# A gated linear attention's gate, projected with tokens on the partitions and multiplied before the transpose

## The chip, the cores and the metric

The kernel runs on one core of a Trainium2 chip. The metric is the device time of one execution in microseconds (us), taken as the median of several runs. A separate execution is recorded by the hardware profiler; its rows name engines as PE (TensorE matmul), PEld (TensorE weight load), DVE (VectorE), ACT (ScalarE), POOL (GpSimd) and SP (SyncE, which issues most DMAs). L94 is line 94 of the kernel.

## The reference

Two layers. Each projects x (256 tokens, 2048 wide) and feeds three groups of heads: A, banded softmax attention of 8 heads; B, gated linear attention (GLA) of 4 heads; M, cross-attention of 4 heads into 256 memory tokens. Each group's output is multiplied by a SiLU gate that is itself a projection of x. The concatenation goes through one output projection, and a layer norm closes the layer. Cut to what matters here:

```python
h = x @ w_in                                   # a_q a_k a_v a_z  b_q b_k b_v b_z b_lr  m_q m_z
y_a = chunk_band_attention(a_q, a_k, a_v)      # 8 heads of 128
o_b = gla_chunk_recurrence(b_q, b_k, b_v, log_g)          # (B, S, 4 heads, 128)
o_b = o_b * rsqrt(mean(square(o_b), axis=-1) + RMS_EPS) * gla_norm_g
y_b = o_b.reshape(B, S, B_WIDTH)               # 512 wide
y_m = memory_attention(m_q, mk, mv)            # 4 heads of 128
y = concatenate([y_a * silu(a_z), y_b * silu(b_z), y_m * silu(m_z)])
x = layer_norm(DEEPNORM_ALPHA * x + y @ w_out)
```

## The kernel before, in words

All matrices are float32. For the large products each operand is split into a high and a low part of the matmul type float32r (`parts`: ACT rounds the high part at L117, DVE subtracts at L118), and three products are added: high times high, low times high, high times low. An operand with features on the partitions is a tile of the pool `opp` (`operand()`, five tiles); four of them hold the layer's x.

Weights come in pieces of 1024 columns of float32 per partition (`piece`): SP loads `raw`, ACT and DVE make `wh` and `wl`; each of the three tags has four buffers. A projection of 512 columns has one of two forms. `ws_group` holds the weights still and streams x, so its result has features on the partitions: two halves of 256 features, each of four pieces (`ws_half`), with two 512-wide and two 256-wide matmuls for each of the 16 blocks of 128 rows and each half. `as_group` holds x still and streams the weights, so its result has tokens on the partitions: eight pieces, with three 512-wide matmuls for each block and each 128 tokens.

The result of a half of `ws_group`, or of a whole `as_group`, is an accumulator `acc` of two PSUM banks from the pool `psd`, which has two of them; the other four banks are the pool `psa` (`bank()`), for the heads. A half is evacuated by `total`: ACT reads one part (L258), DVE adds the other (L259).

PE and SP follow the program's order; ACT, DVE and POOL are put in order by the scheduler that builds the program. The heads are generators that run between the pieces: each piece ends with `tick()`, which takes the next step of a generator that is due.

```python
while waiting and len(active) < 2:
    active.append((waiting.pop(0), 0))
```

At most two are active, the others stand in the list `waiting` in the order they came: the GLA, eight heads of A, four heads of M. A step that yields n is due again n ticks later. `finish` ticks until given generators are done.

In each layer the groups follow one another so: memory keys and values, the GLA's query and key, then values, queries and keys of A, the query of M (MQ), then the four gates BZ, AZ0, AZ1 and MZ, all in the `ws_group` form, then four blocks of the output projection in the `as_group` form. Under the gates run the last heads: the heads of M have three steps each (`m_head`, scores and softmax, transposes, values). The last block of the output projection takes each piece in two DMAs, from a layout split in two parts of 256 columns.

The GLA ends with tokens on the partitions: two tiles `on` of scratch get the outputs (L443), the mean squares (L445), and the factor of the norm (L451); eight transposes (L457) turn them, and ACT multiplies by the norm's gain while it copies them into `yraw` (L459). After a gate group, ACT takes the Silu (L768), DVE multiplies by `yraw` (L772), and `parts` makes the operand of the output projection.

Of the kernel before, what the change touches and what calls it, by code (L numbers as in the profile page):

```python
# [8 lines left out]
F32 = mybir.dt.float32  # L9
# [3 lines left out]
AF = mybir.ActivationFunctionType  # L13
ALU = mybir.AluOpType
# [4 lines left out]
P = 128  # L19
D = 2048  # L20
T = 256
# [11 lines left out]
G_MK, G_MV, G_BQK, G_AQ0, G_AK0, G_AQ1, G_AK1, G_MQ, G_BZ, G_AZ0, G_AZ1, G_MZ, G_WO = range(13)  # L33
# [4 lines left out]
def hybrid_trunk_kernel(  # L38
# [7 lines left out]
    pe, dve, act, pool, sp = nc.tensor, nc.vector, nc.scalar, nc.gpsimd, nc.sync  # L46
# [4 lines left out]
    waiting, active, done, now = [], [], set(), [0]  # L51

    def tick():

        now[0] += 1
        while True:
            while waiting and len(active) < 2:
                active.append((waiting.pop(0), 0))
            due = [e for e in active if e[1] <= now[0]]
            if not due:  # L60
                return
            active.remove(due[0])
            g = due[0][0]
            after = next(g, None)
            if after is not None:
                active.append((g, now[0] + after))
                return
            done.add(g)

    def finish(gens):  # L70
        while not all(g in done for g in gens):
            tick()
# [16 lines left out]
    def nm(s):  # L89
        uid[0] += 1  # L90
        return f"{s}_{uid[0]}"
# [4 lines left out]
    def bank():  # L96
        return psa.tile([P, 512], F32, name=nm("bk"), tag="bk")

    def scratch(shape, dtype=F32):
        return sc.tile(shape, dtype, name=nm("sc"), tag="sc")  # L100

    def small(shape, tag, bufs=1):
        return sm.tile(shape, F32, name=nm(tag), tag=tag, bufs=bufs)

    ident = cst.tile([P, P], F32, name="ident")
# [4 lines left out]
    def operand():  # L110

        x = opp.tile([P, 4, 2, T], F32R, name=nm("x"), tag="x")
        return x[:, :, 0], x[:, :, 1], x.rearrange("p j h t -> p j (h t)")

    def parts(hi, lo, src):

        act.copy(hi, src)  # L117
        dve.tensor_tensor(lo, src, hi.bitcast(F32), op=ALU.subtract)  # L118

    def load_quarter(src):  # L120

        with tc.high_priority(AHEAD):
            raw = wp.tile([P, 4, T], F32, name=nm("raw"), tag="raw")
            x = operand()
            sp.dma_start(raw, src)
            parts(x[0], x[1], raw)
        return x

    def piece(src, n, kp=2):

        with tc.high_priority(AHEAD):
            raw = wp.tile([P, kp, n], F32, name=nm("raw"), tag="raw")
            hi = wp.tile([P, kp, n], F32R, name=nm("wh"), tag="wh")
            lo = wp.tile([P, kp, n], F32R, name=nm("wl"), tag="wl")
            if isinstance(src, list):
                w = n // len(src)
                for i, part in enumerate(src):
                    sp.dma_start(raw[:, :, i * w:(i + 1) * w], part.rearrange("p (k n) -> p k n", k=kp))
            else:
                sp.dma_start(raw.rearrange("p k n -> p (k n)"), src)  # L140
            parts(hi, lo, raw)
        return hi, lo
# [108 lines left out]
    def ws_group(src, xq):  # L251

        for half in range(2):
            acc = ws_half(src[half * 4:half * 4 + 4], xq)
            yield half * 2, acc[:, :, 0], acc[:, :, 1]

    def total(dst, a, b, scale=1.0):
        act.mul(dst, b, scale)  # L258
        dve.scalar_tensor_tensor(dst, a, scale, dst, op0=ALU.mult, op1=ALU.add)  # L259

    def as_products(o, t, xq, w, kt, kk):
        wh, wl = w
        xh, xl, _ = xq[kt // 4]
        j, ts = kt % 4, slice(t * P, (t + 1) * P)
        mm(o, xh[:, j, ts], wh[:, kk], kt == 0, False)
        mm(o, xl[:, j, ts], wh[:, kk], False, False)
        mm(o, xh[:, j, ts], wl[:, kk], False, kt == 15)

    def as_group(src, xq, n, kp=2, first=None):

        acc = psd.tile([P, 2, 512], F32, name=nm("acc"), tag="acc")
        for pc in range(16 // kp):
            if first is not None and pc % 2 == 0:
                xq.append(load_quarter(first[pc // 2]))
            w = piece(src[pc], n, kp)
            for kk in range(kp):
                for t in range(2):
                    as_products(acc[:, t, :n], t, xq, w, pc * kp + kk, kk)
            tick()
        return acc  # L280
# [12 lines left out]
    def gla_inputs(l):  # L293
        gw = small([16, 256], "gw")
        gb = small([P, 2], "gb")
        ng = small([P, 1], "ng")
        pool.dma_start(gw, gate_w[l])
        pool.dma_start(gb, gate_b[l])
        pool.dma_start(ng, norm_g[l])
        return gw, gb, ng  # L300

    def gla(gw, gb, ng, gq, gk, asv, yraw):
# [23 lines left out]
        pt = bank()  # L326
# [53 lines left out]
        pt = bank()  # L380
# [8 lines left out]
        for c in range(3):  # L389
            rs = slice((c % 2) * 64, (c % 2) * 64 + 64)  # L390
            t = c // 2
            for b in range(2):
                for par in range(2):
                    h = 2 * b + par
# [4 lines left out]
        for c in range(3):  # L399
            t = c // 2  # L400
# [17 lines left out]
                ps = slice(half * CH, (half + 1) * CH)  # L418
                act.copy(attn[par][ps, :, ps], pairs[par][ps])
        yield 3  # L420
        on = [scratch([P, 4, P]) for _ in range(2)]
        ms = small([P, 8], "ms")
        sq = scratch([P, P])

# [2 lines left out]
        for par in range(2):  # L427
            for t in range(2):
                for b in range(2):
                    h = 2 * b + par  # L430
                    mm(po[par][:, (t * 2 + b) * P:(t * 2 + b + 1) * P], attn[par][:, t * 2 + b],
                       asv[:, t, 16 + h * P:16 + (h + 1) * P], t == b == 0, False)
        for odd, even in ((1, 2), (3, None)):
            for b in range(2):
                for c in (odd, even):
                    if c is not None:
                        for par in range(2):
                            rs = slice(par * 64, par * 64 + 64)
                            g = (c // 2) * 2 + b
# [9 lines left out]
        rsqrt(rr, ms, 8, 1)  # L449
        for par in range(2):  # L450
            dve.tensor_tensor(on[par], on[par], rr[:, par * 4:par * 4 + 4].unsqueeze(2).to_broadcast([P, 4, P]), op=ALU.mult)  # L451
        yield 2
        for par in range(2):
            pt = bank()
            for t in range(2):
                for b in range(2):
                    pe.transpose(pt[:, b * T + t * P:b * T + (t + 1) * P], on[par][:, t * 2 + b], ident)  # L457
            for b in range(2):
                act.activation(yraw[:, 2 * b + par], pt[:, b * T:(b + 1) * T], AF.Copy, scale=ng[:, 0:1])  # L459

    SCALE = P ** -0.5

# [71 lines left out]
    def transposed(xq):  # L534

        for q in range(4):
            x = operand()
            hi, lo, _ = x
            xq.append(x)
            for j in range(0, 4, 2):  # L540
                pt = bank()
                for jj in range(2):
                    kt = q * 4 + j + jj
                    for t in range(2):
                        pe.transpose(pt[:, jj * T + t * P:jj * T + (t + 1) * P], res[:, t, kt * P:(kt + 1) * P], ident)  # L545
                parts(hi[:, j:j + 2], lo[:, j:j + 2], pt.rearrange("p (j t) -> p j t", j=2))
                yield 2

    def columns(n):
        return slice(n * 512, (n + 1) * 512)  # L550
# [133 lines left out]
    for l in range(L):  # L684
        mk = [per.tile([P, 4, T], F32R, name=nm("mk"), tag=f"mk{i}") for i in range(2)]
        mv = [per.tile([P, 2, 512], F32R, name=nm("mv"), tag=f"mv{i}") for i in range(2)]
        xq = []
# [6 lines left out]
        else:  # L694
            memq = []
            parts(*mv, as_group(w512[l, G_MV], memq, 512, 2, memT))
            gens = [transposed(xq)]
# [7 lines left out]
        yraw = [per.tile([P, 4, T], F32, name=nm("yr"), tag=f"yr{i}") for i in range(4)]  # L705
# [4 lines left out]
        gp = gla_inputs(l)  # L710
# [31 lines left out]
        load_bias(0)  # L742
        load_bias(1)
        gens = [[gla(*gp, gq, gk, asv, yraw[0])]]
        waiting.extend(gens[0])
        for half in range(2):
# [11 lines left out]
        waiting.extend(gens[-1])  # L758


        yq = []
        for i, g in enumerate((G_BZ, G_AZ0, G_AZ1, G_MZ)):
            y = operand()
            gates = []
            for j, a, b in ws_group(w512[l, g], xq):
                sz = scratch([P, 2, T])
                total(sz, a, b)
                act.activation(sz, sz, AF.Silu)  # L768
                gates.append((j, sz))
            finish(gens[i])  # L770
            for j, sz in gates:
                dve.tensor_tensor(sz, sz, yraw[i][:, j:j + 2], op=ALU.mult)  # L772
                parts(y[0][:, j:j + 2], y[1][:, j:j + 2], sz)
            yq.append(y)


        last = l == L - 1
# [3 lines left out]
        for n in range(WO_N):  # L781
            g, b = scratch([P, 512]), scratch([P, 512])
# [19 lines left out]
            acc = as_group(src, yq, 512)  # L802
            for t in range(2):
                add_residual(n, t, acc[:, t], stats)
            if last:
                for t in range(2):
                    r = res[:, t, columns(n)]
# [89 lines left out]
```

## Time and profile before

| | us |
|---|---|
| median of 3 runs | 939.01 (938.53 to 939.02) |
| the profiled execution | 938.5 |
| its span, first to last instruction | 936.4 |
| mean granted TensorE clock | 0.994 of full |

How to read the rows. A row of the timeline has its start in us from the span's start, its length, the engine, the line, the operation, what it writes and reads, shapes and a count, and in brackets how long the engine had been idle before and what released it. Matmul lengths are modelled and overlap, so the distance between two starts is the better measure of pace. A row of the waits has engine, line and what it waited for, then the total, the count and the longest. A row of the windows has the stretch, its length, the busy time and count of PE, PEld, DVE, ACT and POOL, the granted clock, the DMA share and GB/s. In the chain that ended last PE has most of the span, and DMAs were 57.5% of the sixteen engines' time.

### The profile page before, as it was taken

The page shows a single profiled execution, that of the slowest core. Times are in us where ns is not written, and L with a number is a line of the kernel's source. Part 1 is how long each engine was busy: PE and PEld are TensorE (multiplying, and loading weights), DVE is VectorE, ACT ScalarE, POOL GpSimd, SP SyncE. Part 2 cuts the span into 40 slices and gives each one's busy share as a digit, 9 for nine tenths or more (in the row PEclk, how much of TensorE's full clock was granted, in tenths as well). Part 3 has the DMA queues.
Part 4 walks back from the last instruction along what each step waited for, and adds up shares of the span by engine and source line. Part 5 has one row for each costly group of instructions (what it writes and reads, how often), then busy time and mean ns, then how long its engine had stood idle before and what let it go on. Part 6 is the DMA issues. An engine that isn't in the chain of part 4 may idle for free.

```text
span 936.4 us, 14232 instructions
## 1 busy us (share of the span) xinstructions
PE 926.8 (99%) x5520; PEld 813.9 (87%) x5520; DVE 585.6 (63%) x780; ACT 497.8 (53%) x714; POOL 30.1 (3%) x46
## 2 busy tenths in 40 slices
PE   9999999999999999999999999999999999999996
PEld 7889998998888888888888999889888888888884
DVE  5764487555565666555598445965555667566666
ACT  6644474475456665434465346744745576554340
POOL 1000000000000000000041000000000001010000
PEclk9999999999999999999999999999999999999997
DMA  8956855555554466765756475556555554676642
GB/s 290 340 187 175 305 189 168 159 180 175 191 159 157 157 183 199 250 198 183 237 190 225 140 208 177 196 161 186 162 195 163 169 160 155 194 247 204 196 135 90
DMA packets 64723, 178.75 MB, mean 191 GB/s; under 512 B 7016, under 2 KB 22664, under 8 KB 64400
## 3 DMA queue, kind: packets, MB, share of 16 engines
q1 hardware_dynamic: 62928, 173.56, 57.5%
q0 software_dynamic: 1728, 4.28, 1.8%
q8 instruction: 43, 0.70, 0.3%
q14 instruction: 24, 0.20, 0.1%
HBM read 175.69 MB, written 2.10 MB: 190 GB/s over the span
## 4 chain that ended last, share of the span: by engine, by line
PE 94%; DVE 2%; DMA 2%; issue 1%; ACT 0%; SPq 0%; DVEq 0%
PE acc L94 85%; PE bk L94 8%; DMA raw<-memT 1%; PE bk L486 1%; DVE wl L118 0%; PE bk L521 0%; PE bk L545 0%; DVE stats L561 0%; ACT x L117 0%; DVE res L580 0%; DVE res L648 0%; DMA raw<-w 0%; DVE res L560 0%; PE bk L457 0%; DVE x L118 0%
## 5 line engine op out<-in xcount | busy, mean ns | idle before, releaser
L118 DVE TENSOR_TENSOR wl<-raw,wh 128x1024 fp32r<-128x1024 f32 (+3 forms) x325 | 378.3, 1166 | 272.4 <-ACT wh L117 267.9
L117 ACT CAST wh<-raw 128x1024 fp32r<-128x1024 f32 (+3 forms) x325 | 323.3, 996 | 352.9 <-PE acc L94 243.1
L94 PE MATMUL acc<-x,wh 128*128 128x512 f32 x1376 | 439.4, 401 | 0.0
L94 PE MATMUL acc<-wh,x 128*128 128x512 f32 (+1 forms) x1120 | 321.8, 368 | 0.4 <-ACT wh L117 0.4
L94 PEld LDWEIGHTS acc<-x,wl 128*128 128x128 f32 x1376 | 258.4, 188 | 61.2 <-DVE wl L118 0.4
L94 PE MATMUL acc<-x,wl 128*128 128x256 f32 x1376 | 271.4, 279 | 0.0
L94 PEld LDWEIGHTS acc<-wh,x 128*128 128x128 f32 x1120 | 206.1, 188 | 25.5 <-ACT wh L117 1.6
L94 PEld LDWEIGHTS acc<-x,wh 128*128 128x128 f32 x1376 | 211.9, 189 | 2.4 <-issue 0.3
L94 PE MATMUL acc<-wl,x 128*128 128x512 f32 (+1 forms) x560 | 205.8, 368 | 0.1
L94 PEld LDWEIGHTS acc<-wl,x 128*128 128x128 f32 x560 | 105.2, 188 | 13.2 <-DVE wl L118 1.3
L478 ACT ACTIVATE sc<-sc,mx 128x128 f32<-128x128 f32 (+1 forms) x32 | 14.4, 449 | 18.4 <-DVE mx L476 18.4
L259 DVE SCALAR_TENSOR_TENSOR sc<-acc,sc 128x512 f32<-128x512 f32 x23 | 15.7, 683 | 0.0
L471 DVE SCALAR_TENSOR_TENSOR sc<-bk,bias 128x384 f32<-128x384 f32 x16 | 8.9, 555 | 10.8 <-PE bk L94 10.8
L772 DVE TENSOR_TENSOR sc<-sc,yr 128x512 f32<-128x512 f32 x16 | 11.0, 690 | 6.4 <-ACT sc L768 6.4
L560 DVE SCALAR_TENSOR_TENSOR res<-res,acc 128x512 f32<-128x512 f32 x15 | 9.7, 684 | 7.2 <-PE acc L94 7.2
L258 ACT ACTIVATE sc<-acc 128x512 f32<-128x512 f32 x23 | 13.7, 595 | 0.0
L118 DVE TENSOR_TENSOR x<-res,x 128x512 fp32r<-128x512 f32 (+2 forms) x14 | 10.5, 765 | 5.1 <-ACT x L117 5.1
L94 PE MATMUL bk<-qk,qk 128*128 128x128 f32 (+1 forms) x64 | 13.1, 326 | 0.0
L94 PE MATMUL bk<-sc,asv 128*128 128x256 f32 (+1 forms) x64 | 13.0, 326 | 0.0
L768 ACT ACTIVATE sc<-sc 128x512 f32<-128x512 f32 x16 | 10.1, 630 | 4.6 <-DVE sc L259 4.5
L94 PEld LDWEIGHTS bk<-sc,asv 128*128 128x128 f32 x64 | 11.0, 189 | 0.8
L117 ACT CAST x<-res 128x512 fp32r<-128x512 f32 (+2 forms) x14 | 9.2, 679 | 4.7 <-DMA res<-xT 3.2
(175 smaller groups left out, 541.2 us busy)
## 6 DMA issues: line engine op xcount, KB each, us to landing
raw<-w SPq DMA_DIRECT2D x230, 512.0 KB, 3.6
raw<-w SPq DMA_DIRECT2D x64, 388.0 KB, 3.1
raw<-w SPq DMA_DIRECT2D x47, 256.0 KB, 3.2
bias<-relw SPq DMA_DIRECT2D x16, 192.0 KB, 3.8
res<-xT SPq DMA_DIRECT2D x4, 512.0 KB, 5.4
res<-xn SPq DMA_DIRECT2D x1, 2048.0 KB, 7.9
sc<-ln_g POOLq DMA_DIRECT2D x8, 256.0 KB, 4.8
sc<-ln_b POOLq DMA_DIRECT2D x8, 256.0 KB, 5.5
```

Of the source, the lines that this page charges most:

```text
L94: pe.matmul(o, l, r, start=start, stop=stop, skip_group_check=True)
L117: act.copy(hi, src)
L118: dve.tensor_tensor(lo, src, hi.bitcast(F32), op=ALU.subtract)
L258: act.mul(dst, b, scale)
L259: dve.scalar_tensor_tensor(dst, a, scale, dst, op0=ALU.mult, op1=ALU.add)
L471: dve.scalar_tensor_tensor(s, pb[:, :384], SCALE, bias[h], op0=ALU.mult, op1=ALU.add)
L478: act.activation(s[:, own[t]], s[:, own[t]], AF.Exp, bias=mx[:, t:t + 1], accum_out=zs[:, t:t + 1])
L486: pe.transpose(pt[:, i * P:(i + 1) * P], s[:, i * P:(i + 1) * P], ident)
L560: dve.scalar_tensor_tensor(r, r, ALPHA, acc, op0=ALU.mult, op1=ALU.add)
L768: act.activation(sz, sz, AF.Silu)
L772: dve.tensor_tensor(sz, sz, yraw[i][:, j:j + 2], op=ALU.mult)
```

## The change

The gate of the GLA (BZ) is projected by `as_group` in place of `ws_group`: tokens on the partitions. Its weights keep their layout, so each piece is put together by two DMAs. The GLA keeps its normed output untransposed, in `yraw[0]` itself. A new generator, `gla_gated`, takes the Silu of the accumulator straight into scratch, multiplies by the normed output, yields 2, transposes the product and makes the high and the low part of the operand from the transposed bank, with the norm's gain as the factor. It is put into `waiting` behind what stands there after the BZ group; a `finish` before the group and one behind MZ keep the order. The gates AZ0, AZ1 and MZ stay as they are.

```diff
@@ gla
-        on = [scratch([P, 4, P]) for _ in range(2)]
+        on = [yraw[:, 2 * par:2 * par + 2].rearrange("p c (g d) -> p (c g) d", d=P) for par in range(2)]
...
             dve.tensor_tensor(on[par], on[par], rr[:, par * 4:par * 4 + 4].unsqueeze(2).to_broadcast([P, 4, P]), op=ALU.mult)
+
+    def gla_gated(acc, yraw, ng, y):
+
+        sz = [scratch([P, 2, 2, P]) for _ in range(2)]
+        accv = acc.rearrange("p t (b r d) -> p r t b d", b=2, r=2)
+        for par in range(2):
+            act.activation(sz[par], accv[:, par], AF.Silu)
+            on = yraw[:, 2 * par:2 * par + 2].rearrange("p t (b d) -> p t b d", d=P)
+            dve.tensor_tensor(sz[par], sz[par], on, op=ALU.mult)
         yield 2
         for par in range(2):
             pt = bank()
             for t in range(2):
                 for b in range(2):
-                    pe.transpose(pt[:, b * T + t * P:b * T + (t + 1) * P], on[par][:, t * 2 + b], ident)
-            for b in range(2):
-                act.activation(yraw[:, 2 * b + par], pt[:, b * T:(b + 1) * T], AF.Copy, scale=ng[:, 0:1])
+                    pe.transpose(pt[:, b * T + t * P:b * T + (t + 1) * P], sz[par][:, t, b], ident)
+            ptv = pt.rearrange("p (b t) -> p b t", b=2)
+            hi, lo = (x.rearrange("p (b r) t -> p r b t", r=2)[:, par] for x in y[:2])
+            act.activation(hi, ptv, AF.Copy, scale=ng[:, 0:1])
+            dve.scalar_tensor_tensor(lo, ptv, ng[:, 0:1], hi.bitcast(F32), op0=ALU.mult, op1=ALU.subtract)
...
-        yq = []
-        for i, g in enumerate((G_BZ, G_AZ0, G_AZ1, G_MZ)):
+        finish(gens[0])
+        acc = as_group([[w512[l, G_BZ, h * 4 + pc // 2][:, pc % 2 * 512:pc % 2 * 512 + 512] for h in range(2)]
+                        for pc in range(8)], xq, 512)
+        yq = [operand()]
+        gens[0] = [gla_gated(acc, yraw[0], gp[2], yq[0])]
+        waiting.extend(gens[0])
+        for i, g in ((1, G_AZ0), (2, G_AZ1), (3, G_MZ)):
             y = operand()
             gates = []
             for j, a, b in ws_group(w512[l, g], xq):
...
             yq.append(y)
+        finish(gens[0])
```

## The prediction

> **What bounds the kernel now.** I read the page's busy table and its chain first, then the list of waits of PE, then the timeline around the four gate groups.
>
> ```profile
> PE 926.8 (99%) x5520; PEld 813.9 (87%) x5520; DVE 585.6 (63%) x780; ACT 497.8 (53%) x714; POOL 30.1 (3%) x46
> PE 94%; DVE 2%; DMA 2%; issue 1%; ACT 0%; SPq 0%; DVEq 0%
> PE acc L94 <- ACT wh L117: 0.4, 1, 0.4
> ```
>
> PE is busy 99% of the span and 94% of the chain that ended last. The third row is from the list of waits of PE: the only entry for the accumulators of the projections is one wait of 0.4 us, so today no projection ever waits for a free accumulator. ACT and DVE have slack: what the change takes from them is worth nothing by itself. Time changes in two ways only: PE gets other matmuls, or PE is made to wait.
>
> **The matmuls of the gate group.** The old form (`ws_group`) issues 32 units of two 512-wide and two 256-wide matmuls, the new one (`as_group`) 32 units of three 512-wide ones: the same columns. The first two rows are six units apart in an undisturbed gate half, the last two 17 units apart in the output projection, which has the form that the gate now gets.
>
> ```profile
> 344.48 0.62 PE L94 MATMUL acc<-x,wh 128*128 128x512 f32 x2
> ...
> 348.65 0.62 PE L94 MATMUL acc<-x,wh 128*128 128x512 f32 x2
> 381.94 0.62 PE L94 MATMUL acc<-wh,x 128*128 128x512 f32 x2
> ...
> 393.50 0.62 PE L94 MATMUL acc<-wh,x 128*128 128x512 f32 x2
> ```
>
> Old unit: (348.65 - 344.48)/6 = 0.695 us. New unit: (393.50 - 381.94)/17 = 0.680 us. 32 units x 0.015 = 0.5 us a layer, **1.0 us gained** in all.
>
> **Costed at nothing.** The eight transposes of a layer are as many as before, only later (behind the third piece of the second half of AZ1). ACT loses ten instructions a layer and gains four, DVE loses six and gains four; PE hides that, and if PE did not, it would be a gain. Each weight piece now comes as two DMAs, the form of the last output block:
>
> ```profile
> raw<-w SPq DMA_DIRECT2D x230, 512.0 KB, 3.6
> raw<-w SPq DMA_DIRECT2D x47, 256.0 KB, 3.2
> ```
>
> They land no later, four pieces are buffered and PE needs 4 x 0.680 = 2.7 us for one; the output block shows no wait of PE. Without that cover a piece could cost at most 0.5 us (3.2 - 2.7), 8 us in all. The split of the first output operand now waits for the operand tile that MZ's first matmuls of the second half free; three pieces, 8 us, lie between that and its first use.
>
> **The wait that is added.** `psd` has two accumulators. The gate group's result is not read when it is done: it is read by `gla_gated`, which stands in `waiting` behind four cross-attention heads, and only two generators are active. Counting the ticks (each head three steps, 3, 2 and 2 ticks apart) it starts at the fifth piece of AZ1, 13 ticks later; in the built order its two Silu come out right behind the L258 of AZ1's first half. There the accumulators go so: BZ takes the first; AZ0's first half, AZ0's second half and AZ1's first half all take the second, one after the other; AZ1's second half takes the first, once both Silu of `gla_gated` have read it. So at three boundaries a layer PE, which takes its instructions in order, must wait until the half just ended is evacuated, with every later piece and head step queued behind. ACT and DVE keep, around these places, the order of before, so the trace tells when each evacuation ends; before, it lay under the next half's matmuls. The first boundary, AZ0's first half to its second (layer 0):
>
> ```profile
> 313.93 0.40 PE L94 MATMUL acc<-x,wl 128*128 128x256 f32 x2
> 314.16 0.88 PE L94 MATMUL bk<-sc,mv 128*128 128x256 f32 x6
> 314.17 1.05 ACT L117 CAST wh<-raw 128x1024 fp32r<-128x1024 f32 x1 [1.04 <-issue]
> 314.88 0.62 PE L94 MATMUL acc<-x,wh 128*128 128x512 f32 x2
> 315.12 0.59 ACT L258 ACTIVATE sc<-acc 128x512 f32<-128x512 f32 x1
> 315.25 1.23 DVE L118 TENSOR_TENSOR wl<-raw,wh 128x1024 fp32r<-128x1024 f32 x1 [0.66 <-ACT wh L117]
> 316.39 0.69 DVE L259 SCALAR_TENSOR_TENSOR sc<-acc,sc 128x512 f32<-128x512 f32 x1
> ```
>
> The half's last matmuls start at 313.93; a cross-attention head's six follow, and PE wants the accumulator at 314.88. But the half's end frees weight buffers, and ACT and DVE split the next piece (L117, L118) before they read the accumulator (L258, L259): L259 ends at 316.39 + 0.69 = 317.08. Wait: **2.20 us**. The second boundary, AZ0 to AZ1:
>
> ```profile
> 328.18 0.62 PE L94 MATMUL acc<-x,wh 128*128 128x512 f32 x2
> 328.20 1.06 ACT L117 CAST wh<-raw 128x1024 fp32r<-128x1024 f32 x1 [0.87 <-ACT wh L117]
> 329.15 0.46 ACT L513 ACTIVATE sc<-bk,mx 128x256 f32<-128x256 f32 x1
> 329.28 1.23 DVE L118 TENSOR_TENSOR wl<-raw,wh 128x1024 fp32r<-128x1024 f32 x1 [0.23 <-ACT wh L117]
> 330.06 0.59 ACT L258 ACTIVATE sc<-acc 128x512 f32<-128x512 f32 x1
> 331.15 0.68 DVE L259 SCALAR_TENSOR_TENSOR sc<-acc,sc 128x512 f32<-128x512 f32 x1
> ```
>
> No head's matmuls cover this one, and a head's softmax (L513) stands before L258 too: 331.15 + 0.68 - 328.18 = **3.65 us**. The third, AZ1's first half to its second, waits for ACT alone: L258, then two Silu of 512 elements, priced by today's Silu (L768):
>
> ```profile
> 341.68 0.63 PE L94 MATMUL acc<-x,wh 128*128 128x512 f32 x2
> 341.94 0.59 ACT L258 ACTIVATE sc<-acc 128x512 f32<-128x512 f32 x1
> 343.92 0.63 ACT L768 ACTIVATE sc<-sc 128x512 f32<-128x512 f32 x1 [1.13 <-DVE sc L259]
> ```
>
> 341.94 + 0.59 + 2 x 0.63 - 341.68 = **2.11 us**. The same three places in layer 1:
>
> ```profile
> 774.58 0.62 PE L94 MATMUL acc<-x,wh 128*128 128x512 f32 x2
> 776.09 0.69 DVE L259 SCALAR_TENSOR_TENSOR sc<-acc,sc 128x512 f32<-128x512 f32 x1
> 787.88 0.62 PE L94 MATMUL acc<-x,wh 128*128 128x512 f32 x2
> 791.60 0.68 DVE L259 SCALAR_TENSOR_TENSOR sc<-acc,sc 128x512 f32<-128x512 f32 x1
> 801.38 0.63 PE L94 MATMUL acc<-x,wh 128*128 128x512 f32 x2
> 801.63 0.59 ACT L258 ACTIVATE sc<-acc 128x512 f32<-128x512 f32 x1
> ```
>
> 776.09 + 0.69 - 774.58 = 2.20; 791.60 + 0.68 - 787.88 = 4.40 (DVE is later there by a split of layer norm rows); 801.63 + 0.59 + 1.26 - 801.38 = 2.10. Sum of six waits: 2.20 + 3.65 + 2.11 + 2.20 + 4.40 + 2.10 = **16.7 us**. Nothing on PE can fill them.
>
> **What a wait does to the clock.** Before, PE stands still for longer only at the very end, and there the granted clock (the column before the DMA share) falls:
>
> ```profile
> 922.49 0.49 PE L94 MATMUL bk<-gbrow,nparts 4*128 4x512 f32 x1 [0.34 <-ACT nparts L117]
> 924.50:924.75 0.25, 0.00 (x0) 0.00 (x0) 0.25 (x2) 0.00 (x0) 0.00 (x0) 0.76 0.66 254
> 924.75:925.00 0.25, 0.10 (x1) 0.10 (x1) 0.16 (x2) 0.25 (x1) 0.00 (x0) 0.50 0.01 0
> 1.05 3.36 PE L94 MATMUL bk<-zeros 128*128 128x128 f32 x14 [1.05 <-DVE nt L606]
> 4.80 1.22 PE L94 MATMUL acc<-wh,x 128*128 128x512 f32 x2 [0.39 <-ACT wh L117]
> 6.25 0.73 PE L94 MATMUL acc<-wh,x 128*128 128x512 f32 x2
> ```
>
> PE ended a small matmul at 922.98, and the clock halved inside 924.50 to 924.75: some 1.6 us of standstill were enough there, behind a lightly used microsecond. The way back is bounded by the kernel's start: working from 1.05, PE needed 1.22 us for a pair at 4.80 (0.62 later), 0.73 at 6.25; so at most 5.2 us of work at half pace, a loss of 0 to 2.6 us for each fall. I take the middle, 1.3, and grant it to the two longest waits: 2.6 us. [...]
>
> **Sum.** Against the profiled execution's own 938.5 us (span 936.4): 938.5 - 1.0 + 16.7 + 2.6 = 956.8. The median of the runs is 939.0, 0.5 above that execution: 957.3, forecast **957 us**.
>
> **Rivals.**
> - *No fall of the clock*: 939.0 - 1.0 + 16.7 = 954.7. For it: the one fall of the trace came behind a microsecond of light use, and here PE is full up to each wait. Chance 0.25.
> - *The clock falls at all six waits*: 939.0 - 1.0 + 16.7 + 6 x 1.3 = 962.5. For it: 1.6 us sufficed at the end, and the shortest wait is 2.1. Chance 0.15.
> - *The third boundary costs nothing*, if ACT gets to the two Silu before the half ends; then 4.2 less, 953.1 with the two falls, 950.5 without. Against it: in ACT's built order both stand behind the L258 of that very half. Chance 0.08.
> - *Not slower*: if the evacuation ended before PE asks for the accumulator, the waits vanish and the gain of the matmuls remains, 939.0 - 1.0 = 938.0, no change. It decides where L259 ends before the next half's first matmul; in the rows above it ends 2.2 to 4.4 us after it. Chance 0.03.
> - *The doubled DMAs are late in the gate group*: up to 8 us on top, 965. Against it: the output block of that form has no wait. Chance 0.04.
>
> The forecast (two falls) keeps 0.45. 0.2% (1.9 us) is about what a measurement of this kernel can tell from no change: faster 0.01, same 0.03, slower 0.96. The range goes from the third boundary missing without falls (950.5, as 951) to six falls (962.5, as 963); two falls at the dear end of 2.6 each (959.9) lie inside.
>
> **What would show it.** In the changed kernel's waits of PE, `acc L94` should wait for DVE `sc L259` four times (about 2.2, 3.65, 2.2, 4.4 us) and for ACT's Silu of `gla_gated` twice (about 2.1), and PE's idle time should grow by about 17 us, all of it in the two stretches of AZ0 and AZ1. The gate group should take 0.5 us less. The granted clock should dip behind the second boundary of each layer. If PE shows no such waits the argument is wrong at its root; if they are there with other lengths, the order of ACT and DVE at the half's end has moved; if they are as priced and the time is above 958, the clock is it.

## The result, and the profile after

| | before | after |
|---|---|---|
| median, us | 939.01 (938.53 to 939.45) | 962.38 (961.53 to 962.94) |
| profiled execution, its span, us | 938.5, 936.4 | 962.8, 960.7 |
| mean granted clock | 0.994 | 0.987 |

The changed kernel takes 1.0246 times as long (95% interval 1.0232 to 1.0261), 23.4 us more. The forecast of slower was right, and 962.4 lies in the range of 951 to 963, close to its upper end; the forecast itself, 957, is 5.4 us short.

The page of the changed kernel, busy table and chain, as read in the prediction:

```profile
PE 933.5 (97%) x5456; PEld 815.9 (85%) x5456; DVE 582.3 (61%) x776; ACT 489.1 (51%) x698; POOL 30.3 (3%) x46
PE 92%; DVE 3%; DMA 2%; issue 1%; ACT 1%; SPq 0%; DVEq 0%; ACTq 0%
```

PE has fewer instructions (5456 for 5520) and yet is busy 6.7 us longer: at a granted clock of 0.50 its matmuls last longer (the same piece took 4.45 us in place of 2.89 behind the first fall, below). Its idle time grew from 936.4 - 926.8 = 9.6 us to 960.7 - 933.5 = 27.2 us. DVE has one point more of the chain, ACT one point where it had none.

The first rows of the list of waits of PE (engine, tile and line, what it waited for; then total us, count, longest):

```profile
PE acc L94 <- DVE sc L259: 12.0, 4, 4.3
PE acc L94 <- ACT sc L458: 3.4, 2, 1.7
PE acc L94 <- DVE wl L118: 2.1, 2, 1.5
```

The first two rows are the six waits of the prediction, four for DVE and two for the Silu of `gla_gated` (L458 in this kernel). The third is the low part of a weight piece that DVE made late, twice; it was not predicted. Before, the only such row was one wait of 0.4 us.

The timeline at the three boundaries of layer 0, in the order of the prediction: AZ0's first half to its second, AZ0 to AZ1, AZ1's first half to its second.

```profile
313.53 0.87 PE L94 MATMUL bk<-sc,mv 128*128 128x256 f32 x6
313.55 1.05 ACT L117 CAST wh<-raw 128x1024 fp32r<-128x1024 f32 x1 [1.71 <-issue]
314.50 0.59 ACT L258 ACTIVATE sc<-acc 128x512 f32<-128x512 f32 x1
315.77 0.68 DVE L259 SCALAR_TENSOR_TENSOR sc<-acc,sc 128x512 f32<-128x512 f32 x1
316.50 0.76 PE L94 MATMUL acc<-x,wh 128*128 128x512 f32 x2 [2.10 <-DVE sc L259]
...
331.23 0.39 PE L94 MATMUL acc<-x,wl 128*128 128x256 f32 x2
333.33 0.59 ACT L258 ACTIVATE sc<-acc 128x512 f32<-128x512 f32 x1
334.42 0.68 DVE L259 SCALAR_TENSOR_TENSOR sc<-acc,sc 128x512 f32<-128x512 f32 x1
335.15 1.22 PE L94 MATMUL acc<-x,wh 128*128 128x512 f32 x2 [3.54 <-DVE sc L259]
...
350.67 0.87 PE L94 MATMUL bk<-sc,mv 128*128 128x256 f32 x6
351.63 0.59 ACT L258 ACTIVATE sc<-acc 128x512 f32<-128x512 f32 x1
352.12 1.08 ACT L458 ACTIVATE sc<-acc 128x512 f32<-128x512 f32 x2
353.25 0.73 PE L94 MATMUL acc<-x,wh 128*128 128x512 f32 x2 [1.71 <-ACT sc L458]
```

At each boundary the chain is as predicted: the half's last matmuls, ACT's split of the next weight piece (L117), then the reads of the accumulator (L258, L259 or L458), and only then the next half. An undisturbed half follows 0.72 us behind the start of a head's six matmuls, and whatever PE does next follows 0.23 us behind the start of a half's last `wl` pair (both distances from the rows of before: 314.88 - 314.16, 314.16 - 313.93). So the waits, counted in starts, are 316.50 - 313.53 - 0.72 = 2.25 us, 335.15 - 331.23 - 0.23 = 3.69 us and 353.25 - 350.67 - 0.72 = 1.86 us. Layer 1:

```profile
786.66 0.87 PE L94 MATMUL bk<-sc,mv 128*128 128x256 f32 x6
789.63 0.74 PE L94 MATMUL acc<-x,wh 128*128 128x512 f32 x2 [2.10 <-DVE sc L259]
802.81 0.39 PE L94 MATMUL acc<-x,wl 128*128 128x256 f32 x2
807.50 1.22 PE L94 MATMUL acc<-x,wh 128*128 128x512 f32 x2 [4.30 <-DVE sc L259]
822.43 0.87 PE L94 MATMUL bk<-sc,mv 128*128 128x256 f32 x6
825.02 0.73 PE L94 MATMUL acc<-x,wh 128*128 128x512 f32 x2 [1.71 <-ACT sc L458]
```

By the same subtraction 2.25, 4.46 and 1.87 us. The six make 16.4 us.

The rest of the loss is the clock. The windows of the changed kernel behind the six boundaries (stretch, length, busy time of PE, PEld, DVE, ACT, POOL, granted clock, DMA share, GB/s):

```profile
318.00:322.00 4.00, 4.00 (x20) 3.52 (x19) 0.71 (x2) 1.66 (x3) 0.00 (x0) 0.69 0.15 58
334.00:338.00 4.00, 2.85 (x9) 2.46 (x10) 2.48 (x5) 2.47 (x3) 0.00 (x0) 0.52 0.64 211
338.00:342.00 4.00, 4.00 (x18) 3.53 (x17) 0.63 (x1) 1.63 (x2) 0.00 (x0) 0.63 0.00 0
350.00:354.00 4.00, 2.29 (x16) 1.91 (x15) 2.24 (x3) 3.16 (x6) 0.00 (x0) 1.00 0.43 134
788.00:792.00 4.00, 2.37 (x13) 2.10 (x14) 2.43 (x4) 3.02 (x5) 0.00 (x0) 1.00 0.47 169
804.00:808.00 4.00, 0.50 (x1) 0.50 (x2) 3.96 (x8) 3.10 (x8) 0.44 (x1) 0.65 0.52 162
808.00:812.00 4.00, 4.00 (x14) 3.33 (x13) 2.02 (x3) 1.94 (x3) 1.01 (x2) 0.50 0.34 111
824.00:828.00 4.00, 2.98 (x17) 2.63 (x18) 3.15 (x5) 1.94 (x5) 0.65 (x2) 1.00 0.65 136
```

There are three falls in the profiled execution, not two: behind the first and the second boundary of layer 0 and behind the second of layer 1. (Two of the four runs have a mean clock of 0.985 in place of 0.987, so the number need not be the same in all.) Behind the first boundary of layer 1 and both third ones the clock stays at 1.00. What a fall costs is seen in the first piece behind it, four units of four matmuls. These two rows are what follows on PE behind the undisturbed one that starts at 789.63, and behind the one that starts at 316.50:

```profile
792.52 0.28 PE L94 MATMUL bk<-sc,mv 128*128 128x256 f32 x1
320.95 0.41 PE L94 MATMUL bk<-sc,mv 128*128 128x256 f32 x2
```

The one takes 2.89 us, the other 4.45, so 1.6 more. The falls at the second boundaries hold twice as long (6.83 us for 3.42; two 4 us windows in a row are low): the finer windows put them at 334.13 to 340.96 and at 805.17 to 812.00. PE worked from 335.15 and from 807.50, so 5.8 and 4.5 us at half clock (granted 0.50); half of that, 2.9 and 2.2 us, is an estimate of the most that they can have cost. Together at most 6.7 us; the filled kernel below puts the three at 6.1.

The group itself: BZ's first matmuls start at 275.55 before and 275.20 after, AZ0's first at 302.11 and 301.47:

```profile
275.20 0.58 PE L94 MATMUL acc<-wh,x 128*128 128x512 f32 x1
...
301.47 0.39 PE L94 MATMUL acc<-x,wh 128*128 128x512 f32 x1
```

26.27 us for 26.56: it gained 0.3 us, where 0.5 was forecast. The budget of the span: 16.4 (waits) + 6.1 (clock) - 0.6 (matmuls, both layers) = 21.9, against 960.7 - 936.4 = 24.3. Of the 2.4 left, 1.5 is one wait in layer 1, which stands in this trace, but in none of the four kernels below that read the accumulator earlier:

```profile
487.22 2.07 DVE L591 SCALAR_TENSOR_TENSOR res<-res,mvt,sc 128x512 f32<-128x512 f32 x3
489.20 1.22 DVE L118 TENSOR_TENSOR wl<-raw,wh 128x1024 fp32r<-128x1024 f32 x1
490.47 0.50 PE L94 MATMUL acc<-wl,x 128*128 128x512 f32 x1 [1.52 <-DVE wl L118]
```

It is the low part of a weight piece (L118), which DVE makes behind rows of the layer norm (L591), in a group that the change does not touch. Before, DVE has the same order there, and the low part is done at 476.47, 0.05 us ahead of the matmul that takes it: the place has no slack. What made DVE later against PE in this execution is open, and so are the other 0.9 us.

### The profile page after: what moved, and what is told of

It reads as the page before. It is cut to its first block, busy times and chain, and to the rows that moved or that the text cites. A ratio compares the mean times of both kernels' runs of the same rounds, so it can differ in the third digit from the quotient of the medians.

```text
span 960.7 us, 14118 instructions
## 1 busy us (share of the span) xinstructions
PE 933.5 (97%) x5456; PEld 815.9 (85%) x5456; DVE 582.3 (61%) x776; ACT 489.1 (51%) x698; POOL 30.3 (3%) x46
## 4 chain that ended last, share of the span: by engine, by line
PE 92%; DVE 3%; DMA 2%; issue 1%; ACT 1%; SPq 0%; DVEq 0%; ACTq 0%
PE acc L94 84%; PE bk L94 7%; DMA raw<-w 2%; DVE wl L118 1%; ACT wh L117 1%; PE bk L497 1%; PE bk L532 0%; PE bk L556 0%; DVE res L591 0%; DVE res L659 0%; DVE sc L259 0%; ACT sc L458 0%; PE bk L466 0%; DVE sc L527 0%; DVE stats L572 0%
## 5 line engine op out<-in xcount | busy, mean ns | idle before, releaser
L118 DVE TENSOR_TENSOR wl<-raw,wh 128x1024 fp32r<-128x1024 f32 (+3 forms) x325 | 378.1, 1165 | 299.5 <-ACT wh L117 294.9
L117 ACT CAST wh<-raw 128x1024 fp32r<-128x1024 f32 (+3 forms) x325 | 323.3, 996 | 386.1 <-PE acc L94 274.1
L94 PE MATMUL acc<-x,wh 128*128 128x512 f32 x1248 | 403.1, 405 | 15.5 <-DVE sc L259 12.0
L94 PE MATMUL acc<-wh,x 128*128 128x512 f32 (+1 forms) x1248 | 362.8, 372 | 0.1
L94 PEld LDWEIGHTS acc<-x,wl 128*128 128x128 f32 x1248 | 237.1, 190 | 56.6 <-DVE wl L118 0.4
L94 PEld LDWEIGHTS acc<-wh,x 128*128 128x128 f32 x1248 | 229.5, 188 | 29.4 <-ACT wh L117 1.1
L94 PE MATMUL acc<-x,wl 128*128 128x256 f32 x1248 | 248.4, 281 | 0.0
L94 PE MATMUL acc<-wl,x 128*128 128x512 f32 (+1 forms) x624 | 231.1, 370 | 2.1 <-DVE wl L118 2.1
L94 PEld LDWEIGHTS acc<-x,wh 128*128 128x128 f32 x1248 | 194.4, 191 | 19.3 <-DVE sc L259 12.8
L94 PEld LDWEIGHTS acc<-wl,x 128*128 128x128 f32 x624 | 117.3, 188 | 18.1 <-DVE wl L118 3.5
L118 DVE TENSOR_TENSOR x<-res,x 128x512 fp32r<-128x512 f32 (+2 forms) x14 | 10.5, 764 | 6.2 <-ACT x L117 6.2
L259 DVE SCALAR_TENSOR_TENSOR sc<-acc,sc 128x512 f32<-128x512 f32 x19 | 13.0, 683 | 0.0
L117 ACT CAST x<-res 128x512 fp32r<-128x512 f32 (+2 forms) x14 | 9.2, 679 | 5.7 <-DMA res<-xT 4.2
L258 ACT ACTIVATE sc<-acc 128x512 f32<-128x512 f32 x19 | 11.3, 594 | 0.0
L572 DVE BATCH_NORM_STATS2 stats<-res 128x6 f32<-128x512 f32 x16 | 10.9, 686 | 0.1
L259 DVE SCALAR_TENSOR_TENSOR qk<-acc,qk 128x512 f32<-128x512 f32 x16 | 10.9, 682 | 0.0
```

The source lines that it names most:

```text
L94: pe.matmul(o, l, r, start=start, stop=stop, skip_group_check=True)
L572: dve.bn_stats(stats[:, t, n], r)
```

## The experiments

Seven kernels, each compared with the kernel before on the same chip. Its median there was 938.39 us for three of them (the rest last in line, first in line, half filled) and 938.43 us for the other four. The diffs are against the changed kernel, where nothing else is said.

**Read the accumulator at once.** The Silu and the product run right behind the group; only the transposes and the split stay a generator, first in line.

```diff
         gens[0] = [gla_gated(acc, yraw[0], gp[2], yq[0])]
-        waiting.extend(gens[0])
+        next(gens[0][0])
+        waiting.insert(0, gens[0][0])
```

> The changed kernel, but the first step of the gate's generator (both Silu and the product) is emitted right behind the gate's projection, and the rest goes to the head of the waiting list; form, DMAs and transposes stay. Held-accumulator theory: the projections alternate between the two accumulators again, PE has no wait of over 0.5 us on an evacuation, the granted clock stays at 1.00 through the gates, and the time is that of before less the gain of the matmuls: 938.0 (937 to 939.5). Rival, the new form and its two DMAs a piece are what costs: still about 955 to 962.

Measured: 937.89 us (936.58 to 939.15), ratio 0.9995 (0.9986 to 1.0004). Its list of waits of PE has one row left for the accumulators of the projections, for a weight piece:

```profile
PE acc L94 <- ACT wh L117: 0.8, 1, 0.8
```

And its timeline at the first boundary of layer 0:

```profile
312.41 0.88 PE L94 MATMUL bk<-sc,mv 128*128 128x256 f32 x6
313.13 0.63 PE L94 MATMUL acc<-x,wh 128*128 128x512 f32 x2
314.65 0.68 DVE L259 SCALAR_TENSOR_TENSOR sc<-acc,sc 128x512 f32<-128x512 f32 x1
```

PE starts the second half 0.72 us after the head's matmuls, and L259 ends 2.2 us later under it, as before the change. So the whole loss is the held accumulator; the other form of projection, the later product and transposes, and the doubled DMAs together cannot be told from nothing.

**The rest last in line.** As above, but what is left of the generator waits behind the heads.

```diff
         gens[0] = [gla_gated(acc, yraw[0], gp[2], yq[0])]
+        next(gens[0][0])
         waiting.extend(gens[0])
```

> As the kernel that reads the accumulator at once, but the rest of the generator (transposes, split) stays at the end of the waiting list, where the changed kernel has it. Held-accumulator theory: the late transposes cost nothing, 938.0 (937 to 939.5). Rival, the late transposes are a part of the cost: over 940.

Measured: 938.49 us, ratio 1.0000 (0.9990 to 1.0009). One line differs from the changed kernel, and all of the loss is gone: the late place in the line costs nothing once the accumulator is free.

**One DMA for a piece.** The first experiment (read at once), with BZ's weights laid out so that each piece is one DMA of 512 KB. The diff shows what it adds to that experiment.

```diff
-        acc = as_group([[w512[l, G_BZ, h * 4 + pc // 2][:, pc % 2 * 512:pc % 2 * 512 + 512] for h in range(2)]
-                        for pc in range(8)], xq, 512)
+        acc = as_group(w512[l, G_BZ], xq, 512)
...
-            w512[l, g] = halves(wi[:, c:c + 512])
+            w512[l, g] = (pack if g == G_BZ else halves)(wi[:, c:c + 512])
```

> As the kernel that reads the accumulator at once, and the gate's weights laid out so that a piece is one DMA of 512 KB in place of two of 256 KB. Held-accumulator theory: the DMAs were hidden, within 0.5 us of that kernel (about 938.0). Rival, the two DMAs a piece cost: faster than that kernel by more than 1 us.

Measured: 938.05 us, ratio 0.9996 (0.9987 to 1.0005). The 16 additional DMAs a layer are hidden (937.89 us with them).

**First in line, read late.** The change as it is, but `gla_gated` put ahead of the heads in `waiting`.

```diff
-        waiting.extend(gens[0])
+        waiting.insert(0, gens[0][0])
```

> The changed kernel, but the gate's generator goes to the head of the waiting list in place of its end, nothing else. In the built order its two Silu then stand behind AZ0's first half on ACT, so one accumulator is held over one boundary a layer instead of three. Held-accumulator theory: one wait a layer, at AZ0's first half to its second, of about 3.2 us (from the half's end 1.05 + 0.59 of ACT's split and evacuation, 1.28 of table load, 1.1 of the two Silu, less what a head's matmuls cover), none at the other two; 937.9 + 6.4 = 944.3 without falls of the clock, up to 950 with a fall in both layers; I expect 947. Rival, the time hangs on the late transposes and not on the held accumulator: 938.

Measured: 947.22 us (945.66 to 950.25), ratio 1.0098 (1.0078 to 1.0118). A row of its list of waits of PE, and the place in the timeline of layer 0:

```profile
PE acc L94 <- ACT sc L458: 6.3, 2, 3.1
316.81 0.73 PE L94 MATMUL acc<-x,wh 128*128 128x512 f32 x2 [3.14 <-ACT sc L458]
```

First in line is still not at once: two heads are active, and the Silu come out of ACT behind the first half of AZ0, one boundary a layer instead of three. That boundary costs 3.3 us of wait in each layer (at 316.81 and 781.04), and a fall of the clock behind it (317.8 to 321.25 and 782.05 to 785.5).

**The kernel before, with an accumulator held.** The old form of BZ in everything, but the evacuation of its second half is a generator at the end of `waiting`. The diff is against the kernel before.

```diff
+        def late(y, j, a, b):
+            sz = scratch([P, 2, T])
+            total(sz, a, b)
+            act.activation(sz, sz, AF.Silu)
+            dve.tensor_tensor(sz, sz, yraw[0][:, j:j + 2], op=ALU.mult)
+            parts(y[0][:, j:j + 2], y[1][:, j:j + 2], sz)
+            yield 2
...
             for j, a, b in ws_group(w512[l, g], xq):
+                if i == 0 and j == 2:
+                    keep.append(late(y, j, a, b))
+                    continue
...
             yq.append(y)
+            if i == 0:
+                waiting.extend(keep)
+        finish(keep)
```

> The kernel before with its old form of the gate, but the evacuation of the gate's second half (and what follows from it) is a generator at the end of the waiting list, so that this accumulator is held through AZ0 and half of AZ1. The form, the DMAs and the transposes are those of before. Held-accumulator theory: three waits a layer of about 2.2, 3.7 (4.4 in layer 1) and 2.2 us, 17 us in all, and falls of the clock of 3 to 9 us: 962 (958 to 966). Rival, the new form costs: no change from before, 939.

Measured: 966.96 us (961.14 to 968.10), ratio 1.0292 (1.0264 to 1.0319). Its list of waits of PE, and three of the six windows that hold its falls (behind the first, the second and the last wait):

```profile
PE acc L94 <- DVE sc L259: 16.2, 6, 4.3
...
318.50:322.50 4.00, 4.00 (x16) 3.42 (x15) 0.69 (x1) 0.41 (x1) 0.00 (x0) 0.57 0.41 126
335.50:343.00 7.50, 6.22 (x21) 5.42 (x22) 1.91 (x4) 3.02 (x5) 0.00 (x0) 0.54 0.37 128
830.50:834.50 4.00, 4.00 (x16) 3.40 (x16) 2.01 (x4) 1.37 (x4) 0.55 (x1) 0.57 0.53 150
```

The hold alone, with no gate in the new form, gives the loss. The time is 1.0 us above the expected range: here all six waits are followed by a fall (the windows of the other three have 0.57, 0.57 and 0.54). The mean clock of this execution is 0.981, and PE is busy 939.1 us, 12.3 more than before for the same matmuls; the expectation had 3 to 9 us for the falls. One of the four runs, 961.14 us, had a mean clock of 0.988, so the number or the length of the falls differs between executions of one kernel.

**PE kept at work in the waits.** The change as it is, with idle 512-wide matmuls into a spare bank ahead of the three halves: 7, 13 and 6 of them a layer. Their results are not used.

```diff
-    def ws_half(src, xq):
+    def ws_half(src, xq, fill=0):
 
+        if fill:
+            o = bank()
+            for _ in range(fill):
+                mm(o, xq[0][0][:, 0, 0:P], xq[0][2][:, 0], True, True)
...
-            acc = ws_half(src[half * 4:half * 4 + 4], xq)
+            acc = ws_half(src[half * 4:half * 4 + 4], xq, fill[half])
...
-            for j, a, b in ws_group(w512[l, g], xq):
+            for j, a, b in ws_group(w512[l, g], xq, {1: (0, 7), 2: (13, 6), 3: (0, 0)}[i]):
```

> The changed kernel, with idle matmuls of 512 columns into a spare bank ahead of the three projections that wait: 7, 13 and 6 of them a layer, 1.6, 3.0 and 1.4 us at 0.23 us each, inside waits of 2.25, 3.7 and 1.9 us. The results are not used. Theory, waits and clock add: the waits stay as long, counted from the end of the half before, but the clock no longer falls, so 6.5 us less than the changed kernel: 956 (955 to 957.5). Rival, the clock does not matter (the slow matmuls behind the waits have another cause): 962. If a fill outlasts its wait: up to 964.

Measured: 955.94 us (955.47 to 956.13), ratio 1.0186 (1.0170 to 1.0202). The same boundary in its timeline (the added lines move L259 to L263), and one of its windows:

```profile
314.22 1.76 PE L94 MATMUL bk<-x 128*128 128x512 f32 x7
316.48 0.73 PE L94 MATMUL acc<-x,wh 128*128 128x512 f32 x2 [0.50 <-DVE sc L263]
...
334.00:338.00 4.00, 4.00 (x26) 3.55 (x25) 1.78 (x3) 2.41 (x4) 0.00 (x0) 1.00 0.40 126
```

The second half starts at 316.48, as in the changed kernel (316.50): the path through ACT and DVE is untouched, and only the clock is kept: its mean is 0.995, for 0.987 of the changed kernel and 0.994 before. The waits, by the subtraction used above, are 2.26, 3.71, 1.86 us in layer 0 and 2.26, 4.46, 1.86 us in layer 1: filled but not shortened. From BZ's first matmul to the first of the output projection the changed kernel takes 112.47 and 111.10 us in its two layers, the filled one 108.34 and 109.11 us. The difference, 4.1 + 2.0 = 6.1 us, is what the clock costs. The medians say the same, each against its own measurement of the kernel before: 23.4 - 17.5 = 5.9 us.

**Half filled.** The same with 4, 8 and 0 idle matmuls, so that standstills of 1.2 to 2.5 us remain. The diff is against the filled kernel.

```diff
-            for j, a, b in ws_group(w512[l, g], xq, {1: (0, 7), 2: (13, 6), 3: (0, 0)}[i]):
+            for j, a, b in ws_group(w512[l, g], xq, {1: (0, 4), 2: (8, 0), 3: (0, 0)}[i]):
```

> As the kernel with the filled waits, but with 4 idle matmuls (1.0 us) in the first wait, 8 (2.0 us) in the second and none in the third. Standstills left: 1.25, 1.7 (2.5 in layer 1) and 1.9 us. If the clock falls only where PE stands still for about 2 us inside one of the clock's periods of 3.4 us, as the spots of the fall in the changed kernel suggest: at most one fall, 956 to 958.5. Rival, the clock falls with any standstill: three or more falls, 960 or more.

Measured: 955.50 us (954.57 to 957.04), ratio 1.0179 (1.0162 to 1.0196), 0.5 below the expected range. The waits for the Silu in its list of waits of PE (L462 here), then the longest standstill of the profiled execution and the clock behind it:

```profile
PE acc L94 <- ACT sc L462: 3.4, 2, 1.7
...
801.87 0.73 PE L94 MATMUL acc<-x,wh 128*128 128x512 f32 x2 [2.48 <-DVE sc L263]
...
804.00:808.00 4.00, 4.00 (x19) 3.43 (x19) 1.15 (x2) 1.80 (x3) 0.32 (x1) 0.71 0.08 24
```

It is the only fall in the two stretches (802.9 to 806.3). The other five waits, 1.18 to 1.72 us, had none. One of them is what is left of layer 0's second wait (1.72 us; granted 1.00 from 334 to 338, 0.52 in the changed kernel), so a fall was avoided here without filling a wait to its end.

## Why the prediction came out as it did

- *What bounds the kernel*: right. ACT's and DVE's savings are worth nothing, and PE makes the time: its instructions, its waits and, as a third way that "in two ways only" leaves out and the prediction adds later, its clock.
- *The held accumulator*: right in place, cause and size. Six waits at the three boundaries of each layer, for DVE four times and for `gla_gated` twice; 16.4 us for 16.7. Reading the accumulator at once gives back all of the loss, and holding one in the old kernel makes it.
- *The third boundary* was priced 2.11 and 2.10 us and took 1.86 and 1.87: the two Silu from the accumulator took 1.08 us together, where two of today's (L768, from scratch) were added up to 1.26.
- *The matmuls*: 0.3 us a layer for 0.5. The sign is right; the whole is below what the measurement tells, as the two kernels that read at once show (937.89 and 938.05).
- *Costed at nothing*: right for the DMAs (one DMA a piece: 938.05 for 937.89) and for the late transposes (938.49). The late low part of a weight piece at 490.47 is in no step.
- *The clock* is the term that was mis-sized: 2.6 us in the sum, 6.1 by the filled kernel. The steps that failed are the count and the price. Two falls were granted to the two longest waits; there were three, and six in the old kernel with an accumulator held. 1.3 was taken as the middle of 0 to 2.6 for each; measured were 1.6, and 2.5 (4.1 - 1.6) and 2.0 for the two that hold twice as long. That the two longest waits would fall and no other was the author's estimate, and no run shows it: of the two first waits, both 2.25 us, the one of layer 0 had a fall and the one of layer 1 none. The prediction's last sentence named this case: waits as priced and a time above 958, then the clock is it.
- *The rivals*: the one with six falls (962.5) has nearly the measured time, but for another reason, since only three fell, at a higher price. The range reached 963 only by this rival, so it is in part luck that the measured time lies inside. No fall at all is what the filled kernel makes: 955.9, for 954.7 forecast.

## What to carry to other kernels

Here an accumulator was given back when its reader had run, not when its matmuls had ended (962.38 us read late, 937.89 read at once). Before work is deferred, count the buffers that it holds and follow each group behind it to the one that it gets; with two accumulators, one held meant that at each of three boundaries a layer PE waited out the evacuation (1.9 to 4.5 us), and reading it at once, with only the rest deferred, cost nothing (938.49 us, for 938.39 of the kernel before). To such waits the clock is added: here 6.1 us for 16.4 us of waits.

## What the runs showed of the hardware

In the gates of the changed kernel and of the experiments the falls of the clock lasted 3.4 us or 6.8, at a granted clock of 0.50. In the changed kernel the first fall lasts from 317.06 to 320.48, 3.42 us. The clock fell again at 334.13 and rose at 340.96, then fell at 805.17 and rose at 812.00, 6.83 us each time. From 317.06 to 340.96 are 23.90 us, seven times 3.41 us, and from 340.96 to 805.17 are 464.21 us, a seventh of 23.90 taken 136.0 times. That all edges in an execution keep this spacing is the author's estimate from these distances; no run tested it. The finer windows at four of these points:

```profile
320.25:320.50 0.25, 0.25 (x3) 0.15 (x2) 0.00 (x0) 0.00 (x0) 0.00 (x0) 0.54 0.00 0
334.00:334.25 0.25, 0.00 (x0) 0.00 (x0) 0.25 (x2) 0.25 (x1) 0.00 (x0) 0.76 0.88 344
340.75:341.00 0.25, 0.25 (x3) 0.25 (x2) 0.00 (x0) 0.25 (x1) 0.00 (x0) 0.58 0.00 0
805.00:805.25 0.25, 0.00 (x0) 0.00 (x0) 0.25 (x1) 0.25 (x1) 0.00 (x0) 0.84 0.06 11
```

A clock of 0.76 over the 0.25 us from 334.00, with 1.00 ahead and 0.50 behind, puts the fall at 334.13; the other points are read likewise.

In the stretches of the gates PE is full up to each wait (busy 3.42 of the 3.42 us from 310.23, ahead of the first). In the 3.41 us ahead of the three falls of the changed kernel PE stood still for 2.10, 2.51 and 1.97 us (the length of the stretch less the busy time of PE in it). The third waits, 1.71 us of standstill in both layers, had no fall. The first wait of layer 1 had none either, with 2.10 us of standstill like the one of layer 0. In the other kernels, the nine falls of the kernel before with an accumulator held, of first in line and of half filled came behind 3.41 us with 2.10 us of standstill or more, and the waits of half filled with 1.72 us or less had none. So a wait of 2.25 us cost 1.6 us more in layer 0 and nothing in layer 1. If the edges keep the spacing above, one lies at 788.10 and parts the standstill of that wait in layer 1 into 0.6 and 1.5 us; that this spared it is the author's estimate. At the second boundaries PE stood still for another 1.0 and 2.3 us behind the start of the fall (to 335.15 and 807.50), and these are the falls of 6.83 us.

At the end of the kernel before, among small matmuls, the fall for which the prediction read 1.6 us as enough came behind 3.41 us (921.22 to 924.63) that held 2.0 us of standstill, 1.65 behind the small matmul and 0.34 ahead of it. All this was read from the traces; no run shifted a wait by itself.
